# A hybrid decoder trunk in f32: new numbers for the model that orders the instructions, and VectorE in place of GpSimd

## The chip, the cores and the metric

The kernel runs on one core of a Trainium2 chip. The metric is device time in microseconds (us) of one execution; lower is better. The core's engines run their own instruction streams in order and meet through semaphores: TensorE (PE in the rows, PEld its weight loads), VectorE (DVE), ScalarE (ACT), GpSimd (POOL) and SyncE (SP), which here issues the weight transfers.

## The reference

Two layers, each a half-step SwiGLU network, a mixing stage of three branches with gates, and a second half-step SwiGLU network. 256 tokens, model width 1024, everything float32.

```python
for l in range(DEPTH):                       # DEPTH = 2
    h = rms_norm(x, ffn1_norm[l])
    x = x + 0.5 * swiglu(h, ffn1_w_gate[l], ffn1_w_up[l], ffn1_w_down[l])     # hidden 2816
    h = rms_norm(x, mix_norm[l])
    (u, q_b, c_kv, q_i, k_i, w_i, q_c, k_c, v_c, f_c, g_a, g_b, g_c) = split(h @ w_in[l])
    a = s5_branch(u, ...)                    # diagonal state space, 256 wide
    b = dsa_branch(q_b, c_kv, q_i, k_i, w_i, ...)   # 6 heads; an indexer keeps the 64 best keys of a query
    c = fox_branch(q_c, k_c, v_c, f_c)       # 6 heads, attention with forgetting
    merged = sigmoid(g_a) * (a @ w_branch_ssm) + sigmoid(g_b) * (b @ w_branch_dsa) + sigmoid(g_c) * (c @ w_branch_fox)
    x = x + merged @ w_out[l]
    h = rms_norm(x, ffn2_norm[l])
    x = x + 0.5 * swiglu(h, ffn2_w_gate[l], ffn2_w_up[l], ffn2_w_down[l])
return rms_norm(x, final_norm)
```

## The kernel before, in words

**Weights.** All weight matrices are read in the order that `plan` writes down, in units of two tiles of 128 rows by up to 512 columns. SyncE loads a unit into `raw` (four buffers). ScalarE copies it, rounded, into `hi` (`feed_hi`), another engine subtracts to get the rest, `lo = raw - hi` (`feed_lo`). The activations are split the same way (`h0h` and `h0l`, `bh` and `bl`, ...). TensorE then does three matmuls per tile and token half, hi by high part, lo by high part, hi by low part, into the accumulators `ps_acc`. These weight matmuls are nearly all of TensorE's work.

**Small work.** What lies between the big products (the state space scan, the indexer with its top 64, attention, the transposes of a norm) is written as Python generators. Their matmuls go to four scratch banks `ps_t`. `attend` works through three pairs of heads: scores (8 matmuls `ps_t<-kdT,qbT` for the sparse branch, `ps_t<-kcT,qcT` for the forgetting one), four reductions with the bias on VectorE (`st<-ps_t,bm` or `fm`), four exponentials with their sums on ScalarE (`st<-st,mn`), a reciprocal (`ri`), four scalings (`st<-st,ri`), two groups of three transposes (`ps_t<-ident,st`), two copies to `pt`, the value product (`ps_t<-pt,vd` or `pt,vs`), and its split into `bh` (ScalarE) and `bl` (VectorE).

**Who decides the order.** The program is written once, by this Python code, and runs in that order on each engine. `Clock` keeps a planned time for each engine, advanced by `Clock.cost` for every instruction. After each weight tile `Trunk.tick` looks through the generators and advances one, if what it waits for is ready by the planned time and if VectorE and ScalarE are planned no more than `BACKLOG` = 1.25 us past TensorE:

```python
if not self.blocked(g) and self.when(g) <= t["pe"] + EAGER and max(t["dve"], t["act"]) <= now + self.backlog[g]:
    self.step(g)
```

`Trunk.finish` runs given generators to their end and puts no weight matmul between their steps. `mix` calls it for the sparse attention before the product `branch dsa 0`, for the forgetting attention before `branch fox 0`, for the scan before `glu`, and for the transposes of the merged gates before each half of `w_out`. The mixing stage goes through `ORDER`: gate dsa 0, dsa 1, fox 0, fox 1, ssm 0, branch dsa 0, branch fox 0, gate ssm 1, glu, branch dsa 1, ssm 0, fox 1, ssm 1; then come `w_out` and the second network. "Gate" is a product of 1024 by 512 from `h`; "branch" a product of 256 or 384 by 512 from a branch's result, which VectorE multiplies with the gate (`gate<-gate,ps_acc`) and adds to the other branches (`gate<-gate`).

**GpSimd's share.** In the mixing stage a `lo` goes to GpSimd when VectorE is planned over 1 us past TensorE and GpSimd is not (`SPILL`), and so does a gate sum that is not the last one of its half. These are 34 `lo` and 8 gate sums in the two layers. GpSimd also adds the biases of attention (`bm`, `fm`).

All compute instructions stand in the profile at one line, that of the call in `Engine.__getattr__` (L193 before, L212 in the changed kernel), so rows are told apart by their tiles.

Of the kernel before, what the change touches and what calls it, by code (L numbers as in the profile page):

```python
# [9 lines left out]
F32 = mybir.dt.float32  # L10
# [3 lines left out]
OP = mybir.AluOpType  # L14
# [12 lines left out]
HD = 64  # L27
# [35 lines left out]

FEED, PACE = 0.3, 25.0

SPILL = 1.0, 1.5

T_BANKS = 4


# [4 lines left out]
def plan(a):  # L75
# [40 lines left out]
    for l in range(L):  # L116
        ffn(l, "ffn1")
        mix(l)
        ffn(l, "ffn2")
# [3 lines left out]
class Clock:  # L123
# [3 lines left out]
    def __init__(self):  # L127
        self.t = dict.fromkeys(("pe", "dve", "act", "pool", "dma"), 0.0)
        self.done = {}

    def ready(self, ap, eng=None):
        t, by = self.done.get(ap.tensor.name, (0.0, eng))
        return t + (SAME if by == eng else LATENCY)

    def put(self, eng, cost, outs, ins):
        start = max([self.t[eng]] + [self.ready(x, eng) for x in ins])
        self.t[eng] = start + cost
        for x in outs:
            done = start + cost + (1.8 if eng == "dma" else 0)
            self.done[x.tensor.name] = max(self.done.get(x.tensor.name, (0.0, eng)), (done, eng))  # L140
# [4 lines left out]
    def late(self, eng, cost, out, src):  # L145
        self.t[eng] += 1.0
        self.done[out.tensor.name] = max(self.t[eng], self.ready(src)) + cost + 3.0, "dma"

    @staticmethod
    def cost(eng, op, out, aps, kw):  # L150
        n = 1
        for d in out.shape[1:]:
            n *= d
        if eng == "pe":
            if op == "transpose":
                return 0.107
            return ((4 if aps[1].shape[0] > HD else 2) if aps[1].dtype == F32 else 1) * max(n / 2380, out.shape[0] / 1200)
        scalars = sum(x.shape[1:] == (1,) or list(x.shape[1:]) == [1] for x in aps[2:])
        if eng == "act":
            return 0.05 + n / 1200 + 0.045 * scalars + (0.13 if "accum_out" in kw else 0)  # L160
        if eng == "pool":
            return 0.14 + n * (2.15e-3 if op == "tensor_tensor" else 3.4e-3 if scalars else 1.15e-3)
        if op == "tensor_tensor_reduce":
            scalars = 0
        if op in ("max", "match_replace"):
            n = max(x.shape[-1] for x in aps)
        fast = op in ("tensor_scalar", "tensor_copy", "memset") and not any("ps_" in x.tensor.name for x in aps)
        return 0.07 + n * (0.52e-3 if fast else 1.04e-3) + 0.06 * scalars


class Engine:
# [3 lines left out]
    def __getattr__(self, op):  # L175
        f = getattr(self.eng, op)

        def call(*args, **kw):
            aps = [x for x in list(args) + list(kw.values()) if isinstance(x, bass.AP)]
            if op == "dma_start":  # L180
                n = 4
                for d in args[0].shape:
                    n *= d
                if self.name == "sp":
                    self.clock.put("dma", n / 360e3, aps[:1], aps[1:])
                else:
                    self.clock.late(self.name, n / 360e3, aps[0], aps[1])
            elif aps:
                outs = aps[:1] + [x for k, x in kw.items() if k == "accum_out"]
                if op == "tensor_tensor_reduce":  # L190
                    outs.append(aps[-1])
                self.clock.put(self.name, Clock.cost(self.name, op, aps[0], aps, kw), outs, aps[1:])
            return f(*args, **kw)  # L193

        return call
# [14 lines left out]
class Trunk:  # L210
    def __init__(self, ctx, tc, a, out):
        self.clock = Clock()  # L212
        self.tc, self.nc, self.a, self.out = tc, Engines(tc.nc, self.clock), a, out
        self.ctx = ctx
        nc = self.nc
        pool = lambda **kw: ctx.enter_context(tc.tile_pool(**kw))

        self.const = pool(name="const", bufs=1, side="right")
        self.rawp = pool(name="raw", bufs=RAW_BUFS, side="right")
        self.small = pool(name="small", bufs=2, side="right")  # L220
        self.hpool = pool(name="h", bufs=1, side="left")
        self.piecep = pool(name="piece", bufs=1, side="left")
        self.accp = pool(name="acc", bufs=4, space=PSUM)
        self.tp = pool(name="tps", bufs=T_BANKS, space=PSUM)
        self.dram = pool(name="scratch", bufs=2, space=DRAM)
        self.tlive, self.tcount = {}, 0
        self.bg, self.wait, self.rank, self.due, self.backlog = [], {}, {}, {}, {}
        self.spill = False

        self.units = plan(a)  # L230
        self.raw, self.split_tiles, self.freed = {}, {}, {}
        self.n_dma = self.n_hi = self.n_lo = self.n_used = 0
# [53 lines left out]
    def feed(self):  # L286

        now, ready = self.clock.t["pe"] + FEED, self.clock.ready
        while self.n_hi < min(self.n_used + HI_AHEAD, self.n_dma) and ready(self.raw[self.n_hi]) <= now:
            self.feed_hi(self.n_hi + 1)  # L290
        while self.n_lo < min(self.n_used + LO_AHEAD, self.n_hi) and ready(self.split_tiles[self.n_lo]) <= now:
            self.feed_lo(self.n_lo + 1)
# [40 lines left out]
    def feed_lo(self, upto):  # L333
        nc = self.nc
        while self.n_lo < min(upto, len(self.units)):
            i = self.n_lo
            _, nk, n = self.units[i]
            self.feed_hi(i + 1)
            src, hi = self.raw.pop(i)[:, :nk, :n], self.split_tiles[i]
            lo = self.piecep.tile([P, 2, 512], F32R, tag="lo", name="lo", bufs=LO_AHEAD + 1)  # L340
            t = self.clock.t
            eng = nc.gpsimd if self.spill and t["dve"] > t["pe"] + SPILL[0] and t["pool"] < t["pe"] + SPILL[1] else nc.vector
            eng.tensor_tensor(lo[:, :nk, :n], src, hi[:, :nk, :n].bitcast(F32), op=OP.subtract)
            self.split_tiles[i] = (hi, lo)
            self.freed[i] = self.clock.ready(lo)
            self.n_lo += 1
            self.feed_dma(i + 1 + RAW_BUFS)
# [320 lines left out]
    def mix(self, l, nxt):  # L668
        nc, tc = self.nc, self.tc
        a = self.a  # L670
# [3 lines left out]
        with tc.tile_pool(name="mix", bufs=1, side="left") as pool:  # L674
# [72 lines left out]
            gate, merged, left = {}, [None, None], [3, 3]  # L747
            mgens = []
            self.new = [None, None]
            for kind, name, d in ORDER:  # L750
                if kind == "gate":
                    g = gate[name, d] = pool.tile([P, 2, 512], F32, tag="gate", name="gate", bufs=5)
                    pg = self.acc()
                    for k0 in (0, 4):
                        self.mm_tok(pg, self.hx, k0, 4, 512, 0, 7)
                    for t in range(2):
                        nc.scalar.activation(g[:, t], pg[t], AF.Tanh, scale=rhalf[:, t:t + 1])
                    continue
                if kind == "glu":
                    self.finish(gen_s)  # L760
                    self.ssm_T = self.glu()
                    continue
                if name != "ssm":
                    self.finish(*((gen_x,) if name == "dsa" else (gen_g, gen_f)))
                hi, lo = getattr(self, f"{name}_T")
                nk = BRANCH_K[name]
                pb = self.acc()
                self.mm_tok(pb, lambda k: (hi[:, k], lo[:, k]), 0, nk, 512, 0, nk - 1)
                g = gate[name, d]
                left[d] -= 1  # L770
                for t in range(2):
                    nc.vector.scalar_tensor_tensor(g[:, t], g[:, t], 1.0, pb[t], op0=OP.add, op1=OP.mult)
                    if merged[d] is not None:
                        m = merged[d][:, t]
                        (nc.gpsimd if left[d] else nc.vector).tensor_tensor(m, m, g[:, t], op=OP.add)
                if merged[d] is None:
                    merged[d] = g
                if not left[d]:
                    self.new[d] = self.new_hT(d)
                    mgens.append(self.spawn(self.norm_T(merged[d], None, self.new[d]), -1))  # L780
# [593 lines left out]
    def run(self):  # L1374
        nc, tc, a = self.nc, self.tc, self.a
# [13 lines left out]
        for l in range(L):  # L1389
            with tc.tile_pool(name="prep", bufs=1, side="right") as pp:  # L1390
# [17 lines left out]
                gens.append(self.spawn(self.prep_layer(l, pp, *gens[:1]), 0, PREP))  # L1408
                self.ffn(C_MIX + 8 * l)
                self.finish(*gens)  # L1410
            self.spill = True
            self.mix(l, C_FFN2 + 8 * l)
            self.spill = False
            if l == L - 1:
                self.fn, self.y = self.late("fin", [P, D]), self.late("y", [P, 2, D])
                nc.gpsimd.dma_start(self.fn, a["final_norm"].rearrange("(o d) -> o d", o=1).partition_broadcast(P))
# [73 lines left out]
```

## Time and profile before

| | |
|---|---|
| device time, median of 3 runs | 1224.71 us (1224.34 to 1225.38) |
| the profiled execution | 1230.51 us |
| its span, first to last instruction | 1228.7 us |
| mean granted TensorE clock (1 is 2.4 GHz) | 0.979 |
| TensorE busy | 1177.6 us, 96% of the span |
| VectorE, ScalarE, GpSimd busy | 804.6, 601.8, 197.9 us |

The busy times are sums over the span; engines work beside each other. The profiled execution is 5.80 us longer than the median, of which 1.8 us lie outside its span. The granted clock has two levels in the rows, 1.00 and 0.50 (2.4 and 1.2 GHz).

### The profile page before, as it was taken

To read this page: it belongs to the slowest core of one execution; us is meant where nothing else is said; L and a number is where in the kernel's file an instruction comes from. 1 tells how busy PE (TensorE), PEld (TensorE's weight loads), DVE (VectorE), ACT (ScalarE), POOL (GpSimd) and SP (SyncE) were. 2 spreads that over 40 slices of the span, in tenths; PEclk is the share of its full clock that TensorE was granted. 3 is DMA by queue.
4 is the path that set the end of the run, shared out by engine and by line. 5 is a ranking of instruction groups with operands and counts; after the bars stand their busy time and mean duration, and the time that the engine had idled before them with its cause. 6 is when DMAs were issued, how large, how long until landed. Compare 5 with 4: busy or idle time off the path is not lost.

```text
span 1228.7 us, 16525 instructions
## 1 busy us (share of the span) xinstructions
PE 1177.6 (96%) x5976; PEld 986.1 (80%) x5976; DVE 804.6 (65%) x1335; ACT 601.8 (49%) x883; POOL 197.9 (16%) x192
## 2 busy tenths in 40 slices
PE   5999999997999999999999999998899999999996
PEld 4887888896868788888888888888777778888885
DVE  6987555699656775555576655557985576555554
ACT  4444444643665464444455445445365545544442
POOL 4116000153401380000000000012450130000000
PEclk8999999898999999999999999999899999999998
DMA  7765465444435656647655656554543455665661
GB/s 238 219 186 166 142 217 165 142 138 128 147 103 175 200 182 188 188 121 241 189 177 168 176 155 213 188 151 130 163 146 106 145 192 179 202 185 166 197 191 67
DMA packets 114898, 208.07 MB, mean 169 GB/s; under 512 B 7454, under 2 KB 26544, under 8 KB 114816
## 3 DMA queue, kind: packets, MB, share of 16 engines
q1 hardware_dynamic: 113024, 202.80, 53.1%
q0 software_dynamic: 1504, 3.81, 1.1%
q8 instruction: 47, 0.77, 0.3%
q10 hardware_dynamic: 288, 0.39, 0.1%
q14 instruction: 35, 0.29, 0.1%
HBM read 205.91 MB, written 1.07 MB: 168 GB/s over the span
## 4 chain that ended last, share of the span: by engine, by line
PE 85%; DVE 10%; ACT 2%; issue 1%; DMA 1%; SPq 0%; DVEq 0%; ACTq 0%
PE ps_acc L193 78%; PE ps_t L193 7%; DVE lo L193 2%; DVE score L193 2%; DVE gate L193 1%; DMA raw<-in_ffn_w_gate_dram 1%; DVE ft L193 1%; DVE m L193 1%; ACT u L193 1%; ACT hi L193 1%; DVE state L193 1%; ACT vT L193 0%; DVE rsqt L193 0%; DVE g L193 0%; SPq L193 0%
## 5 line engine op out<-in xcount | busy, mean ns | idle before, releaser
L193 ACT ACTIVATE hi<-raw 128x1024 fp32r<-128x1024 f32 (+3 forms) x415 | 410.9, 991 | 467.7 <-PE ps_acc L193 397.3
L193 DVE TENSOR_TENSOR lo<-raw,hi 128x1024 fp32r<-128x1024 f32 (+4 forms) x381 | 445.6, 1173 | 291.0 <-PE ps_acc L193 245.3
L193 PE MATMUL ps_acc<-hi,h0h 128*128 128x512 f32 (+3 forms) x544 | 218.1, 401 | 5.7 <-ACT hi L193 5.6
L193 PE MATMUL ps_acc<-lo,h0h 128*128 128x512 f32 (+3 forms) x544 | 210.0, 386 | 6.7 <-DVE lo L193 6.7
L193 PE MATMUL ps_acc<-hi,h0l 128*128 128x512 f32 (+3 forms) x544 | 209.7, 385 | 0.0
L193 PE MATMUL ps_acc<-hi,h1h 128*128 128x512 f32 (+3 forms) x544 | 209.6, 385 | 0.0
L193 PE MATMUL ps_acc<-hi,h1l 128*128 128x512 f32 (+3 forms) x544 | 204.8, 376 | 0.0
L193 PE MATMUL ps_acc<-lo,h1h 128*128 128x512 f32 (+3 forms) x544 | 204.7, 376 | 0.0
L193 PE MATMUL ps_acc<-hi,ath 128*128 128x512 f32 x352 | 138.0, 392 | 0.0
L193 PE MATMUL ps_acc<-hi,atl 128*128 128x512 f32 x352 | 137.1, 390 | 0.0
L193 PE MATMUL ps_acc<-lo,ath 128*128 128x512 f32 x352 | 137.0, 389 | 0.0
L193 PEld LDWEIGHTS ps_acc<-lo,h0h 128*128 128x128 f32 x544 | 106.0, 195 | 24.7 <-DVE lo L193 7.9
L193 PEld LDWEIGHTS ps_acc<-hi,h0h 128*128 128x128 f32 x544 | 105.8, 195 | 24.2 <-ACT hi L193 6.2
L193 PEld LDWEIGHTS ps_acc<-hi,h0l 128*128 128x128 f32 x544 | 105.8, 194 | 20.1 <-DVE h0l L193 0.6
L193 PEld LDWEIGHTS ps_acc<-hi,h1h 128*128 128x128 f32 x544 | 103.2, 190 | 19.7 <-issue 2.6
L193 PEld LDWEIGHTS ps_acc<-hi,h1l 128*128 128x128 f32 x544 | 103.0, 189 | 18.2
L193 PEld LDWEIGHTS ps_acc<-lo,h1h 128*128 128x128 f32 x544 | 103.2, 190 | 17.1 <-issue 0.5
L193 POOL TENSOR_TENSOR lo<-raw,hi 128x1024 fp32r<-128x1024 f32 (+3 forms) x34 | 72.9, 2154 | 193.7 <-PE ps_acc L193 99.3
L193 PEld LDWEIGHTS ps_acc<-hi,atl 128*128 128x128 f32 x352 | 66.1, 188 | 13.9
L193 PEld LDWEIGHTS ps_acc<-lo,ath 128*128 128x128 f32 x352 | 66.1, 188 | 13.3
L193 PEld LDWEIGHTS ps_acc<-hi,ath 128*128 128x128 f32 x352 | 66.1, 188 | 13.3
L193 POOL DMA_DIRECT2D wuk<-in_dsa_w_uk_dram x4 | 2.2, 560 | 459.6 <-PE ps_acc L193 358.4
(281 smaller groups left out, 1360.1 us busy)
## 6 DMA issues: line engine op xcount, KB each, us to landing
raw<-in_ffn_w_down_dram SPq DMA_DIRECT2D x88, 512.0 KB, 4.2
raw<-in_ffn_w_up_dram SPq DMA_DIRECT2D x80, 512.0 KB, 3.6
raw<-in_ffn_w_gate_dram SPq DMA_DIRECT2D x79, 512.0 KB, 3.6
raw<-in_w_in_dram SPq DMA_DIRECT2D x56, 512.0 KB, 3.5
raw<-in_w_out_dram SPq DMA_DIRECT2D x16, 512.0 KB, 3.8
raw<-in_ffn_w_gate_dram SPq DMA_DIRECT2D x18, 256.0 KB, 2.8
raw<-in_ffn_w_up_dram SPq DMA_DIRECT2D x16, 256.0 KB, 2.8
raw<-in_w_in_dram SPq DMA_DIRECT2D x16, 256.0 KB, 2.8
```

The source lines that it names most:

```text
L193: return f(*args, **kw)
```

## The change

The numbers of `Clock.cost` are replaced for all four compute engines. `Clock.shared` and a list `held` are new: they let the plan hold a VectorE instruction back while a GpSimd instruction that reads the same ports is planned, and the other way round. `SPILL` goes: every `lo` is VectorE's, and so is every gate sum. The core of the diff:

```diff
     def put(self, eng, cost, outs, ins, shared=False):
         start = max([self.t[eng]] + [self.ready(x, eng) for x in ins])
+        if shared:
+            for a, b in self.held["pool" if eng == "dve" else "dve"]:
+                if a <= start < b:
+                    start = b
+            self.held[eng] = self.held[eng][-8:] + [(start, start + cost)]
         self.t[eng] = start + cost
...
         if eng == "pe":
...
-            return ((4 if aps[1].shape[0] > HD else 2) if aps[1].dtype == F32 else 1) * max(n / 2380, out.shape[0] / 1200)
+            if aps[1].dtype == F32:
+                return (1 if aps[1].shape[0] > HD else 0.5) * (0.01 + max(n, out.shape[0]) / 600)
+            return 0.0135 + max(n / 2400, out.shape[0] / 1200)
...
         if eng == "act":
-            return 0.05 + n / 1200 + 0.045 * scalars + (0.13 if "accum_out" in kw else 0)
+            return 0.2 + n / 1205 + 0.03 * scalars
...
-        return 0.07 + n * (0.52e-3 if fast else 1.04e-3) + 0.06 * scalars
+        return 0.155 + n * (0.52e-3 if fast else 1.04e-3) + (0.06 * scalars if n > 16 else 0)
+
+    @staticmethod
+    def shared(eng, op, aps):
+
+        if eng == "pool":
+            return op != "memset"
+        ins = [x for x in aps[1:] if "ps_" not in x.tensor.name and x.shape[1:] != (1,) and list(x.shape[1:]) != [1]]
+        fast = op in ("tensor_scalar", "tensor_copy") and len(ins) == len(aps) - 1 and "ps_" not in aps[0].tensor.name
+        return eng == "dve" and (fast or len(ins) > 1)
...
-            t = self.clock.t
-            eng = nc.gpsimd if self.spill and t["dve"] > t["pe"] + SPILL[0] and t["pool"] < t["pe"] + SPILL[1] else nc.vector
-            eng.tensor_tensor(lo[:, :nk, :n], src, hi[:, :nk, :n].bitcast(F32), op=OP.subtract)
+            nc.vector.tensor_tensor(lo[:, :nk, :n], src, hi[:, :nk, :n].bitcast(F32), op=OP.subtract)
...
-                        (nc.gpsimd if left[d] else nc.vector).tensor_tensor(m, m, g[:, t], op=OP.add)
+                        nc.vector.tensor_tensor(m, m, g[:, t], op=OP.add)
```

The new numbers move instructions in all of the mixing stage, in both layers alike. The first place is TensorE at the end of gate ssm 0 and the start of branch dsa 0 (`bh` and `bl` are the split result of the sparse attention). Before, one product follows the other:

```order
L193 MATMUL ps_acc<-hi,h1h 128x512
L193 MATMUL ps_acc<-lo,h1h 128x512
L193 MATMUL ps_acc<-hi,h1l 128x512
L193 MATMUL ps_acc<-hi,bh 128x512
L193 MATMUL ps_acc<-lo,bh 128x512
L193 MATMUL ps_acc<-hi,bl 128x512
```

In the changed kernel, TensorE has this between them; the scores of the first pair alone stand earlier, among the gate's matmuls:

```order
L212 MATMUL ps_t<-ident,st 128x128 x3
L212 MATMUL ps_t<-kdT,qbT 128x256 x2
L212 MATMUL ps_t<-kdT,qbT 128x128 x2
L212 MATMUL ps_t<-ident,st 128x128 x3
L212 MATMUL ps_t<-pt,vd 64x256 x2
L212 MATMUL ps_t<-pt,vd 64x128 x2
L212 MATMUL ps_t<-ident,st 128x128 x6
L212 MATMUL ps_t<-pt,vd 64x256 x2
L212 MATMUL ps_t<-pt,vd 64x128 x2
L212 MATMUL ps_t<-kdT,qbT 128x256 x2
L212 MATMUL ps_t<-kdT,qbT 128x128 x2
...
L212 MATMUL ps_t<-ident,st 128x128 x6
```

Where three dots stand, four scores of the first forgetting pair follow, and behind the last row the third value product and then the first matmul with `bh`. Before, the three value products stood 79 and 49 rows apart among the gates' weight matmuls, the last one 74 rows ahead of the end of gate ssm 0.

The second place is TensorE between branch dsa 0 and branch fox 0. Before, their matmuls, which have the same names, follow each other without a break; in the changed kernel the forgetting attention, of which only the scores of two pairs stand earlier, is here as one piece:

```order
L212 MATMUL ps_acc<-hi,bl 128x512
L212 MATMUL ps_t<-ident,st 128x128 x6
L212 MATMUL ps_t<-pt,vs 64x256 x2
L212 MATMUL ps_t<-pt,vs 64x128 x2
L212 MATMUL ps_t<-ident,st 128x128 x6
L212 MATMUL ps_t<-pt,vs 64x256 x2
L212 MATMUL ps_t<-pt,vs 64x128 x2
L212 MATMUL ps_t<-kcT,qcT 128x256 x2
L212 MATMUL ps_t<-kcT,qcT 128x128 x2
L212 MATMUL ps_t<-ident,st 128x128 x6
L212 MATMUL ps_t<-pt,vs 64x256 x2
L212 MATMUL ps_t<-pt,vs 64x128 x2
```

So six steps of attention stand without a weight matmul among them, where none did. On VectorE, in both places, `bl` of a pair stands ahead of the reductions of the next pair (of two of the four, for the second forgetting pair).

The third place is VectorE at the end of the mixing stage, from the multiplication of branch fox 1 to the first half of `w_out` (`h0l` is the low part of the first transposed half of the merged gates). Before:

```order
L193 SCALAR_TENSOR_TENSOR gate<-gate,ps_acc 128x512 x2
L193 TENSOR_TENSOR lo<-raw,hi 128x1024
L193 SCALAR_TENSOR_TENSOR h0l<-ps_t,h0h 128x512 x2
L193 SCALAR_TENSOR_TENSOR gate<-gate,ps_acc 128x512
L193 TENSOR_TENSOR gate<-gate 128x512
L193 SCALAR_TENSOR_TENSOR gate<-gate,ps_acc 128x512
L193 TENSOR_TENSOR gate<-gate 128x512
L193 TENSOR_TENSOR lo<-raw,hi 128x1024
```

And in the changed kernel:

```order
L212 SCALAR_TENSOR_TENSOR gate<-gate,ps_acc 128x512
L212 TENSOR_TENSOR gate<-gate 128x512
L212 SCALAR_TENSOR_TENSOR gate<-gate,ps_acc 128x512
L212 TENSOR_TENSOR gate<-gate 128x512
L212 TENSOR_TENSOR lo<-raw,hi 128x1024
L212 SCALAR_TENSOR_TENSOR gate<-gate,ps_acc 128x512
L212 TENSOR_TENSOR gate<-gate 128x512
L212 SCALAR_TENSOR_TENSOR gate<-gate,ps_acc 128x512
L212 TENSOR_TENSOR gate<-gate 128x512
L212 SCALAR_TENSOR_TENSOR h0l<-ps_t,h0h 128x512 x2
```

The two sums of fox 1 have come over from GpSimd, and `h0l` has moved from ahead of the last branch's four instructions to behind them. On TensorE the eight transposes for `h0h` and `h0l` moved with it, behind the last weight matmul of the last branch. At the start of the second network a like thing is seen: `h0l` stood between the two pairs of additions to `x`, and stands now behind both, on ScalarE `h0h` behind the squares of the second pair.

## Rows read from the trace of the kernel before

**Rows 1.** The page, busy time of each engine over the span.

```profile
PE 1177.6 (96%) x5976; PEld 986.1 (80%) x5976; DVE 804.6 (65%) x1335; ACT 601.8 (49%) x883; POOL 197.9 (16%) x192
```

**Rows 2.** Waits of TensorE: us in total, times, longest us.

```profile
PE ps_t L193 <- DVE qbT L193: 9.8, 2, 6.1
...
PE ps_t L193 <- ACT qk L193: 5.0, 2, 2.5
PE ps_t L193 <- ACT st L193: 4.1, 2, 2.0
PE ps_t L193 <- DVE cn L193: 3.5, 2, 1.9
PE ps_t L193 <- DVE ft L193: 3.3, 2, 1.7
PE ps_t L193 <- DVE gate L193: 3.2, 4, 0.8
```

**Rows 3.** Busy time by window; the last columns: granted clock, DMA share, GB/s.

```profile
238.60:245.40 6.80, 5.78 (x24) 5.39 (x25) 2.84 (x6) 2.90 (x5) 0.00 (x0) 0.50 0.02 6
245.40:286.40 41.00, 34.47 (x272) 33.35 (x270) 40.31 (x98) 16.86 (x27) 18.93 (x9) 1.00 0.42 125
286.40:296.60 10.20, 7.08 (x22) 5.44 (x23) 9.94 (x26) 2.67 (x9) 3.39 (x3) 0.50 0.43 145
344.40:347.80 3.40, 3.40 (x9) 2.66 (x10) 2.00 (x12) 3.04 (x11) 0.00 (x0) 0.51 0.49 154
680.00:720.00 40.00, 40.00 (x182) 33.15 (x181) 22.43 (x26) 18.79 (x21) 0.00 (x0) 1.00 0.61 175
842.80:846.20 3.40, 3.40 (x12) 3.40 (x12) 3.37 (x7) 1.06 (x1) 0.00 (x0) 0.50 0.04 6
```

**Rows 4.** The page, GpSimd's `lo`: busy us, mean ns, idle before.

```profile
L193 POOL TENSOR_TENSOR lo<-raw,hi 128x1024 fp32r<-128x1024 f32 (+3 forms) x34 | 72.9, 2154 | 193.7 <-PE ps_acc L193 99.3
```

**Rows 5.** Groups of VectorE by form, 228 to 420 us: busy us, mean ns.

```profile
L193 DVE TENSOR_TENSOR lo<-raw,hi 128x1024 fp32r<-128x1024 f32 x32 | 41.8, 1310 | 20.8 <-PE ps_acc L193 18.4 <-ACT hi L193 1.7 <-issue 0.6
L193 DVE SCALAR_TENSOR_TENSOR gate<-gate,ps_acc 128x512 f32<-128x512 f32 x12 | 7.8, 679 | 0.1
L193 DVE TENSOR_TENSOR gate<-gate 128x512 f32<-128x512 f32 x4 | 6.3, 1564 | 0.4
...
L193 DVE COPY pt<-ps_t 128x384 f32<-128x384 f32 x7 | 3.9, 553 | 0.3 <-PE ps_t L193 0.2
```

**Rows 6.** Timeline: start us, us, engine, line, op, tiles, count.

```profile
287.88 1.65 PE L193 MATMUL ps_t<-kdT,qbT 64*128 64x256 f32 x8 [6.13 <-DVE qbT L193]
...
311.09 0.49 PE L193 MATMUL ps_t<-ident,st 128*128 128x128 f32 x3
...
311.50 0.92 PE L193 MATMUL ps_t<-kdT,qbT 64*128 64x256 f32 x8
...
312.57 0.29 DVE L193 CUSTOM_DVE_ANT_0 st<-ps_t,bm 128x128 f32<-128x128 f32 x1
...
312.96 0.40 ACT L193 ACTIVATE st<-st,mn 128x128 f32<-128x128 f32 x1
...
314.64 0.19 ACT L193 ACTIVATION_READ_ACCUMULATOR st<-st,mn 128x1 f32 x1
...
342.35 0.17 DVE L193 RECIPROCAL ri<-rs 128x4 f32<-128x4 f32 x1
342.55 0.40 ACT L193 ACTIVATE st<-st,ri 128x128 f32<-128x128 f32 x1 [0.91 <-DVE ri L193]
...
343.00 0.55 PE L193 MATMUL ps_t<-ident,st 128*128 128x128 f32 x3 [2.04 <-ACT st L193]
...
352.91 0.87 PE L193 MATMUL ps_t<-pt,vd 128*64 128x256 f32 x8
...
353.83 0.39 ACT L193 ACTIVATE bh<-ps_t 128x256 fp32r<-128x256 f32 x1
...
354.25 0.42 DVE L193 TENSOR_TENSOR bl<-ps_t,bh 128x256 fp32r<-128x256 f32 x1 [0.94 <-ACT bh L193]
```

More of the change, by code (lines that the diff above doesn't have):

```diff
@@ L64 @@
 FEED, PACE = 0.3, 25.0
-SPILL = 1.0, 1.5
 T_BANKS = 4
@@ L129, in __init__ @@
         self.done = {}
+        self.held = {"dve": [], "pool": []}
     def ready(self, ap, eng=None):
@@ L133, in ready, with put @@
         return t + (SAME if by == eng else LATENCY)
-    def put(self, eng, cost, outs, ins):
+    def put(self, eng, cost, outs, ins, shared=False):
         start = max([self.t[eng]] + [self.ready(x, eng) for x in ins])
+        if shared:
[3 more added lines that the diff above has]
+            self.held[eng] = self.held[eng][-8:] + [(start, start + cost)]
         self.t[eng] = start + cost
@@ L156, in cost @@
                 return 0.107
-            return ((4 if aps[1].shape[0] > HD else 2) if aps[1].dtype == F32 else 1) * max(n / 2380, out.shape[0] / 1200)
+            if aps[1].dtype == F32:
+                return (1 if aps[1].shape[0] > HD else 0.5) * (0.01 + max(n, out.shape[0]) / 600)
+            return 0.0135 + max(n / 2400, out.shape[0] / 1200)
         scalars = sum(x.shape[1:] == (1,) or list(x.shape[1:]) == [1] for x in aps[2:])
         if eng == "act":
-            return 0.05 + n / 1200 + 0.045 * scalars + (0.13 if "accum_out" in kw else 0)
+            return 0.2 + n / 1205 + 0.03 * scalars
         if eng == "pool":
-            return 0.14 + n * (2.15e-3 if op == "tensor_tensor" else 3.4e-3 if scalars else 1.15e-3)
+            return 0.16 + n * (2.2e-3 if op == "tensor_tensor" else 3.4e-3 if scalars else 0.8e-3 if op == "memset" else 2e-3)
         if op == "tensor_tensor_reduce":
@@ L166, in cost @@
             n = max(x.shape[-1] for x in aps)
-        fast = op in ("tensor_scalar", "tensor_copy", "memset") and not any("ps_" in x.tensor.name for x in aps)
-        return 0.07 + n * (0.52e-3 if fast else 1.04e-3) + 0.06 * scalars
+        if op == "tensor_tensor_scan":
+            return 0.155 + n * 2e-3
+        fast = op in ("tensor_scalar", "tensor_copy", "memset") and not any("ps_" in x.tensor.name for x in aps) and n > 128
+        return 0.155 + n * (0.52e-3 if fast else 1.04e-3) + (0.06 * scalars if n > 16 else 0)
[6 more added lines that the diff above has]
+        return eng == "dve" and (fast or len(ins) > 1)
 class Engine:
@@ L191, in call @@
                     outs.append(aps[-1])
-                self.clock.put(self.name, Clock.cost(self.name, op, aps[0], aps, kw), outs, aps[1:])
+                self.clock.put(self.name, Clock.cost(self.name, op, aps[0], aps, kw), outs, aps[1:],
+                               Clock.shared(self.name, op, aps))
             return f(*args, **kw)
@@ L227, in __init__ @@
         self.bg, self.wait, self.rank, self.due, self.backlog = [], {}, {}, {}, {}
-        self.spill = False
         self.units = plan(a)
@@ L1410, in run @@
                 self.finish(*gens)
-            self.spill = True
             self.mix(l, C_FFN2 + 8 * l)
-            self.spill = False
             if l == L - 1:
```

## The prediction

> **What bounds the kernel now.** I read the page's busy times first: TensorE works 1177.6 of 1228.7 us, no other engine over two thirds [rows 1]. So time can only be won where TensorE stands still or runs slowly, and lost where it is made to. TensorE's waits come next. Apart from the start of the program, which the new order leaves as it was, they are all for small work of the mixing stage: 9.8, 5.0, 4.1, 3.5 and 3.3 us over both layers, together 25.7, and 3.2 for the gate sums ahead of `w_out` [rows 2]. Then the windows around these waits: they show a granted clock of 0.50, the 1.2 GHz level, behind a wait or a thinning of the work, with 5.78, 7.08 and 3.40 us of TensorE work in them in layer 0 and 3.40 in the first of layer 1 [rows 3]; layer 1 repeats the second and third. That is 30.1 us of work at half speed, so 15.1 us lost. At most 25.7 + 15.1 = 40.8 us can come back from the mixing stages; the gate wait is taken separately below.
>
> VectorE is the engine that is late there: 40.31 of 41.0 us busy from 245.4 to 286.4, with GpSimd busy 18.93 beside it [rows 3]. It works slower beside GpSimd. A gate sum, 128x512, takes 1564 ns on the mean, the multiplication of the same size 679 [rows 5].
>
> **The change, part by part.** I give the cost for one layer; both layers' mixing stages have the same new order.
>
> *What it removes.* GpSimd's 34 `lo` took 72.9 us [rows 4]. On VectorE the 17 of a layer cost at most 1.31 each, 22.3, and the four gate sums .68 each, as the multiplication of that size [rows 5]; 25 us more instructions per layer, partly repaid by undisturbed ones. The order also puts off much small work: the first sparse scores come 184 rows later on TensorE. So VectorE and ScalarE have room early, and I expect the five waits of the stage's first half to go. I take the whole 40.8 us as returned, the most that the rows allow; the lower end is that half stays, 20.4.
>
> *A, the sparse block.* What is put off has to be done by `finish`, with nothing for TensorE to do between. At the end of gate ssm 0 nearly three pairs of attention now stand in one piece (the first `order` rows). Each pair's value product depends on a chain through three engines. From the start of one value product: .92 to `bh`, .42 to `bl`, .42 for `bl` itself, then the next pair's first reduction, which stands behind it on VectorE, .39 to its exponential, 1.87 from the first exponential to the end of the last sum (312.96 to 314.83), .20 for the reciprocal, .45 from scaling to transposes, about .5 for the other head's scaling, .55 for its transposes, .55 for the copy: 6.3 us, of which I take 6.2, as some of it starts early [rows 5, 6]. The third pair's scores stand behind the second value product, and its reductions start 1.07 after them (311.50 to 312.57), so it takes about 6.4. With 2.8 for what is left of the first pair and .87 for the last product: 16.3 us at full clock. At half clock scores take 1.65 instead of .92 [rows 6]; I add .9 a pair, which is 19.0. TensorE's own work in it at full clock is six groups of transposes (.41 from one start to the next), three scores (.92) and three value products (.87), 7.8 us. The block therefore adds 8.5 us at full clock, 11.2 at half. I take 11.2: waits of 2.48 to 6.13 us are what stands ahead of the half clock in the rows, and this block is made of such waits.
>
> *B, the forgetting block.* The same ahead of branch fox 0, with only one pair of scores inside: 2.8 + 5.2 + 6.4 + .87 = 15.3 at full clock (5.2, as two reductions with their exponentials are done earlier), and as it begins slowly, 19.4. TensorE's own work: 6 x .41 + .92 + 3 x .87 = 6.0. It adds 9.3 or 13.4; I take 13.4.
>
> No row of before shows such a block. From below, if the pairs overlapped fully, each would cost what its busiest engine does, about 3 us (four exponentials 1.87, scalings, `bh`), and both blocks would add almost nothing; `bl` ahead of the next reductions excludes that. From above, GpSimd's bias additions may disturb VectorE in them; with one and a half times what a gate sum lost (1564 - 679 = 885 ns) that is 1.3 to 1.4 a block.
>
> *C, the clock behind the blocks.* The rows have 5.78 and 7.08 us of work at 0.50 behind waits. I take 6 us behind each block, 3 lost each: 6.0. The Trainium skill says, in TensorE: Matmul & The Clock Gate, section HAM oscillation, that a stream of matmuls broken by waits falls back to half rate and that every stretch starts cold again; the trace agrees, with 0.50 from 286.4 to 296.6 behind a wait of 6.13 us. By that rule gathering work into blocks costs twice, as I have it; by the full-clock reading (below) it would cost the waits alone.
>
> *D, ahead of `w_out`.* The last branch is 12 weight matmuls of .22 (40.0 us for 182 rows [rows 3]), 2.6 us. In them VectorE now does fox 1's four instructions (4 x .68 = 2.7) and a `lo` (1.31), so it is 1.4 us behind at their end; the last branch's four follow (2.7), and the transposes of both halves stand behind them. TensorE waits about 4.0 instead of 1.6 (four gate waits, 3.2 in two layers [rows 2]): +2.4. Behind such a wait I take 3.40 us of work at half clock: +1.7.
>
> *E, at the second network's start.* `h0l` behind two more additions and a square, three operations of 128x512 at about .65: +1.9.
>
> Sum for a layer: 11.2 + 13.4 + 6.0 + 2.4 + 1.7 + 1.9 = 36.6. For two 73.2, less 40.8: +32.4 us. The durations come from the profiled execution of 1230.51 us (span 1228.7), which would become 1262.9; set against the median, 1224.7 + 32.4 = **1257 us**.
>
> **The rivals.**
>
> *The clock holds.* The blocks' own matmuls may be enough to keep the clock at 1.00. Then A is 8.5, B 9.3, C nothing, D 2.4 and E 1.9: 22.1, twice 44.2, less 40.8: +3.4, about 1228. For it: the waits for `cn` [rows 2], one of which lies in the window from 245.4 to 286.4, leave that window at 1.00 [rows 3]. Against it: 0.50 behind the wait of 6.13 [rows 3, 6].
>
> *Faster: VectorE is no longer disturbed, and the blocks are cheap.* This is one mechanism: with GpSimd quiet, the 128-wide scalings and sums run at their undisturbed length, small work lands where the new plan puts it, and each block is covered. If all of the blocks' cost disappeared, 1224.7 - 40.8 = 1184; it decides for faster when the new cost is under 20.4 us a layer, just below the 22.1 that full clock gives. For it speaks the gate sum's 1564 against 679 ns. Against it: no weight matmul stands in the blocks, so nothing covers them. The Trainium skill, SBUF — State Buffer, section Who interferes with whom, calls the ports that VectorE shares with GpSimd an exclusive lock: an instruction that comes second waits for the whole of the other. The trace agrees, with that 1564 beside 679; by that rule taking GpSimd out gains whatever the order is.
>
> *VectorE is overloaded.* If its 25 us more a layer find no room, the `lo` come late and weight matmuls wait. It was busy 40.31 of 41.0 us in the worst stretch. If some 20 us a layer come onto the path: 1257 + 40 = 1297. Against it: small work of that stretch has been put off.
>
> *The change does nothing:* gains and blocks even out, within 2.4 us of before; it needs a cost of 20.4 a layer, by chance alone.
>
> **How the numbers follow.** Forecast .70; clock holds .14; VectorE overloaded .07; faster .06; even .03. The forecast's own range is 1244 (half of what half clock adds to A and B, and half of C: 6.4 a layer less) to 1277 (1.4 more in each block, and a third of the 40.8 not returned: 5.6 + 13.6 more). To hold 8 in 10 it takes in the clock rival: 1227 to 1277. About 0.2%, 2.4 us, is what a measurement of this kernel can tell from no change. Faster by more: .06, and .02 of the clock rival, .08. Within: .03, and .04 of the clock rival, .07. Slower: .85.
>
> **What would show each step.** The waits for `qk`, `cn`, `kdT`/`qbT` and `ft` gone or smaller; the gate sums on VectorE near .69. Ahead of branch dsa 0 and branch fox 0 a stretch of 16 to 20 us without a weight matmul, in which TensorE waits for `pt`, `st` and `mn`, with the clock at 0.50 in and behind it; some 4 us of waiting for `gate` ahead of `w_out`; a mean clock below 0.979. The prediction is wrong if the blocks last under 10 us, if the clock stays at 1.00, or if waits for `lo` come up among the gates.

## The result, and the profile after

The changed kernel takes 1252.08 us (1250.54 to 1253.74, 4 runs), against 1224.64 us: 1.0223 times as long, 95% interval 1.0206 to 1.0241. Forecast were 1257 us and slower. The profiled executions differ by 23.2 us (1253.74 against 1230.51); their spans, 1251.9 and 1228.7, by the same.

The page's first row, the counterpart of [rows 1]:

```profile
PE 1189.2 (95%) x5976; PEld 993.5 (79%) x5976; DVE 798.3 (64%) x1381; ACT 602.6 (48%) x879; POOL 101.2 (8%) x150
```

GpSimd's work is halved, and VectorE, with 46 instructions more, is busy 6.3 us less. TensorE does the same 5976 instructions in 11.6 us more. So half of the 23.2 us shows as longer TensorE work, and the other 11.6 as idle time. The split is rough: a row of several matmuls can hold a wait inside it, as the second value product below does. The waits of TensorE (us in total, times, longest), to be held against [rows 2]:

```profile
PE ps_t L212 <- ACT st L212: 23.9, 8, 3.7
...
PE ps_acc L212 <- DVE h0l L212: 6.2, 2, 3.1
...
PE ps_t L212 <- DVE st L212: 5.9, 5, 1.6
PE ps_acc L212 <- ACT h0h L212: 3.5, 4, 1.5
```

The rows for `qbT`, `qk`, `cn`, `ft` and `gate` are gone. What stands there now is attention: 23.9 + 5.9 us of waiting for scaled scores (`st`), and 6.2 + 3.5 for the transposed halves ahead of `w_out` (`h0l`) and of the second network (`h0h`). VectorE's groups, 228 to 445 us, answer to [rows 5]:

```profile
L212 DVE TENSOR_TENSOR lo<-raw,hi 128x1024 fp32r<-128x1024 f32 x46 | 58.1, 1269 | 25.7 <-PE ps_acc L212 15.7 <-issue 8.0 <-ACT hi L212 1.7
L212 DVE SCALAR_TENSOR_TENSOR gate<-gate,ps_acc 128x512 f32<-128x512 f32 x12 | 8.0, 679 | 0.0
L212 DVE TENSOR_TENSOR gate<-gate 128x512 f32<-128x512 f32 x8 | 5.5, 692 | 0.3
```

A gate sum takes 692 ns where it took 1564, and VectorE has time to spare, 25.7 us ahead of the large `lo` alone. It is not the bound. The two blocks of layer 0 in windows (us, busy time of each engine; the last three columns are granted clock, DMA share and GB/s):

```profile
333.94:339.00 5.06, 3.47 (x23) 1.94 (x21) 2.15 (x8) 2.32 (x7) 0.00 (x0) 1.00 0.26 95
340.20:346.60 6.40, 5.26 (x24) 3.45 (x26) 2.64 (x6) 1.57 (x5) 1.41 (x2) 0.51 0.00 0
347.00:349.60 2.60, 0.40 (x6) 0.19 (x2) 1.54 (x11) 2.14 (x9) 0.00 (x0) 1.00 0.00 0
350.40:353.60 3.20, 3.20 (x14) 1.91 (x13) 1.11 (x5) 1.60 (x6) 0.00 (x0) 0.55 0.03 5
353.80:357.20 3.40, 3.40 (x20) 2.52 (x19) 1.58 (x6) 2.00 (x6) 1.42 (x2) 1.00 0.33 72
363.50:373.50 10.00, 7.20 (x30) 4.32 (x28) 3.42 (x12) 2.65 (x8) 0.00 (x0) 0.50 0.00 0
377.60:380.80 3.20, 3.20 (x13) 1.82 (x12) 0.67 (x2) 0.86 (x3) 0.00 (x0) 0.54 0.00 0
381.00:384.40 3.40, 3.40 (x17) 2.75 (x16) 2.40 (x4) 1.58 (x2) 0.00 (x0) 1.00 0.22 49
418.40:421.80 3.40, 3.40 (x12) 2.67 (x12) 1.22 (x2) 0.50 (x1) 0.00 (x0) 0.54 0.42 122
```

The busy times are those of PE, PEld, DVE, ACT and POOL. In the 6.4 us from 340.2 TensorE has 5.26 us of work, at half clock, VectorE 2.64 and ScalarE 1.57; in the 2.6 us from 347.0 TensorE has 0.40, the other two 1.54 and 2.14. It is a chain, in which one engine waits for the other. One turn of it, from the second value product of the sparse block to the next transposes, on the timeline:

```profile
343.09 2.25 PE L212 MATMUL ps_t<-pt,vd 128*64 128x256 f32 x8
...
345.27 1.47 PE L212 MATMUL ps_t<-kdT,qbT 64*128 64x256 f32 x8
345.38 0.38 ACT L212 ACTIVATE bh<-ps_t 128x256 fp32r<-128x256 f32 x1 [2.34 <-PE ps_t L212]
345.79 0.42 DVE L212 TENSOR_TENSOR bl<-ps_t,bh 128x256 fp32r<-128x256 f32 x1 [2.05 <-ACT bh L212]
...
346.89 0.29 DVE L212 CUSTOM_DVE_ANT_0 st<-ps_t,bm 128x128 f32<-128x128 f32 x1 [0.67 <-PE ps_t L212]
...
349.32 0.40 ACT L212 ACTIVATE st<-st,ri 128x128 f32<-128x128 f32 x1 [0.24 <-DVE ri L212]
...
349.78 0.45 PE L212 MATMUL ps_t<-ident,st 128*128 128x128 f32 x1 [2.38 <-ACT st L212]
```

The value product takes 2.25 us here where it took .87 [rows 6], the scores 1.47 instead of .92. Not all of this is the clock: the first value product of the block, at a granted clock of 1.00, takes 1.58 (at 335.93, shown below), as the third of its eight matmuls starts .7 us behind the first, where it was .3 before. Then ScalarE (`bh`), VectorE (`bl` and the reductions), ScalarE (exponentials), VectorE (reciprocal) and ScalarE (scaling) follow until the transposes at 349.78.

### The profile page after: what moved, and what is told of

Same layout as the page of the kernel before. It is cut to its first block, busy times and chain, and to the rows that moved or that the text cites. A ratio compares the mean times of both kernels' runs of the same rounds, so it can differ in the third digit from the quotient of the medians.

```text
span 1251.9 us, 16455 instructions
## 1 busy us (share of the span) xinstructions
PE 1189.2 (95%) x5976; PEld 993.5 (79%) x5976; DVE 798.3 (64%) x1381; ACT 602.6 (48%) x879; POOL 101.2 (8%) x150
## 5 line engine op out<-in xcount | busy, mean ns | idle before, releaser
L212 DVE TENSOR_TENSOR lo<-raw,hi 128x1024 fp32r<-128x1024 f32 (+3 forms) x415 | 473.4, 1147 | 282.6 <-PE ps_acc L212 209.0
L212 PE MATMUL ps_acc<-hi,h0h 128*128 128x512 f32 (+3 forms) x544 | 213.6, 393 | 9.8 <-ACT hi L212 6.2
L212 PE MATMUL ps_acc<-lo,h0h 128*128 128x512 f32 (+3 forms) x544 | 207.2, 381 | 5.9 <-DVE lo L212 5.9
L212 PE MATMUL ps_acc<-hi,h1h 128*128 128x512 f32 (+3 forms) x544 | 206.4, 379 | 0.0
L212 PEld LDWEIGHTS ps_acc<-lo,h1h 128*128 128x128 f32 x544 | 102.5, 188 | 17.2 <-issue 0.2
L212 PE MATMUL ps_t<-ident,st 128*128 128x128 f32 x72 | 17.5, 380 | 30.1 <-ACT st L212 23.9
L212 DVE SCALAR_TENSOR_TENSOR act<-ps_acc,rstd,s 128x512 f32<-128x512 f32 (+1 forms) x48 | 32.1, 705 | 18.6 <-PE ps_acc L212 18.6
```

## The experiments

Ratios are to the kernel before, measured beside each of the three groups of runs: 1225.75 us for the kernels of experiments 1, 2 and the 0.07 of experiment 3, 1226.70 for its other two, the first kind of fillers and the first kernel of experiment 5, 1226.15 for the rest. The intervals behind the ratios are of 95%.

**1. The engine move alone, and the numbers alone.** The first kernel is the one before with the move:

```diff
-            t = self.clock.t
-            eng = nc.gpsimd if self.spill and t["dve"] > t["pe"] + SPILL[0] and t["pool"] < t["pe"] + SPILL[1] else nc.vector
-            eng.tensor_tensor(lo[:, :nk, :n], src, hi[:, :nk, :n].bitcast(F32), op=OP.subtract)
+            nc.vector.tensor_tensor(lo[:, :nk, :n], src, hi[:, :nk, :n].bitcast(F32), op=OP.subtract)
...
-                        (nc.gpsimd if left[d] else nc.vector).tensor_tensor(m, m, g[:, t], op=OP.add)
+                        nc.vector.tensor_tensor(m, m, g[:, t], op=OP.add)
```

> The kernel before with every lo and every gate sum on VectorE, and its old cost numbers. The order has no block of sparse attention left and one short piece of five rows of forgetting attention. Theory (the loss comes from the order that the new numbers make, with attention in pieces that nothing covers): 1205 to 1228 us, not slower than before; no waits of 2 to 4 us for st ahead of branch dsa 0 and branch fox 0. Rival (VectorE is overloaded by the 17 lo and 4 sums that a layer adds to it): 1240 us or more, with TensorE waiting for lo or gate among the gates.

1224.58 us, 0.9995 (0.9983 to 1.0008): no change. The waits of the first half are smaller, but the order differs, and it has waits of its own:

```profile
PE ps_acc L193 <- DVE h0l L193: 6.4, 2, 3.2
...
PE ps_t L193 <- ACT pt L193: 5.0, 6, 2.0
PE ps_t L193 <- ACT st L193: 3.4, 2, 1.7
PE ps_t L193 <- ACT qk L193: 3.4, 2, 2.0
```

VectorE is not overloaded by the work: no wait for `lo` but those of the program's start. The second kernel is the changed one with the two edits above undone.

> The changed kernel with its new cost numbers and its model of shared ports, but with the rule that sends lo to GpSimd and the gate sums on GpSimd as before. The order has the forgetting block whole (11 rows) and the sparse one in part (6 rows instead of 16). Theory (order): 1238 to 1255 us, most of the loss stays: the forgetting block's 15 us a layer, and some 6 of the sparse one. Rival (the engine move makes the loss): 1220 to 1230.

1231.92 us, 1.0047 (1.0031 to 1.0064). Slower by 6 us, so the numbers cost time without the move, but less than I expected: the stretch with the 11 rows of the forgetting block lasts 14.7 us here (354.94 to 369.59), where it lasts 21.5 in the changed kernel. The two halves of the change do not add up: 0 and +6 us alone, +27 together. The order points to the reason: 16 rows stand in the sparse block instead of 6. With VectorE's 25 us more a layer, its planned time should lie further behind TensorE's, and more attention is left to `finish`; the planned times themselves are not on record.

**2. How far VectorE may be behind.** The changed kernel with one number changed:

```diff
-TICK, BACKLOG, PREP, EAGER = 1.5, 1.25, 0.0, -0.5
+TICK, BACKLOG, PREP, EAGER = 1.5, 8.0, 0.0, -0.5
```

> The changed kernel with one number changed: BACKLOG 8 us in place of 1.25, so that generators go on although VectorE or ScalarE is planned far behind. The order has no attention block; small work stands earlier. Theory (order): the 32 us of a layer's blocks and their neighbours go; 1190 to 1228, as waits of the first half may come back in part. Rival (the blocks are not the cause, VectorE's load is): 1245 or more.

1225.66 us, 0.9987 (0.9968 to 1.0006). The blocks are gone, and 26 us with them, but the old waits are back; TensorE's in total:

```profile
PE ps_acc L212 <- DVE lo L212: 11.3, 6, 5.3
PE ps_t L212 <- DVE qbT L212: 8.8, 2, 4.4
```

About 5 of the 11.3 for `lo` lie outside the program's start. The clock has a share too. Behind the wait for `qbT` in layer 0 it stands at 0.50 for 23.9 us, with TensorE busy nearly all the time:

```profile
282.72:306.62 23.90, 23.40 (x89) 20.57 (x90) 12.00 (x37) 7.07 (x22) 6.86 (x6) 0.50 0.22 67
```

Between too little and too much small work ahead of the gates there must be a better place.

**3. VectorE's planned cost.** One line of the changed kernel, the planned cost of most instructions of VectorE, whose fixed part is 0.155 us:

```diff
-        return 0.155 + n * (0.52e-3 if fast else 1.04e-3) + (0.06 * scalars if n > 16 else 0)
+        return 0.04 + n * (0.52e-3 if fast else 1.04e-3) + 0.06 * scalars
```

In the first of the three kernels 0.07 stands there, which makes it the line of the kernel before, in the others 0.10 and 0.04. The condition `n > 16` goes in all three, so they differ from each other in one number, but from the changed kernel in two things.

> The changed kernel with VectorE's old cost formula alone (0.07 us per instruction in place of 0.155). The order has the sparse attention spread again and a forgetting block of 8 rows (three value products, scores earlier) in place of 11. Theory (order; VectorE's fixed cost is what puts small work off): the sparse block's 12 us a layer go, the forgetting one costs 12 to 15 still: 1224 to 1236. Rival (VectorE's load, not its planned cost): 1245 or more.

> The changed kernel with VectorE's planned cost per instruction 0.10 us in place of 0.155 (0.07 ran at 1216). By the order the forgetting block is whole (11 rows), the sparse one has 6 rows (two pairs, scores done). Theory (the order's blocks set the time): between the two, 1224 to 1240. Rival (the loss grows evenly with the number, or comes from another of the new numbers): 1216 as with 0.07, or 1245 and more.

> The changed kernel with VectorE's planned cost per instruction 0.04 us. The order has no attention block at all. Theory (blocks): the 1.5 us waits for st that 0.07 still has go: 1206 to 1217, if small work put earlier does not make the old waits for qk, cn and qbT come back; with them 1217 to 1228. Rival (VectorE's load is what counts): 1245 or more.

| planned cost, us | rows in the two blocks, sparse and forgetting | the two stretches without a weight matmul, layer 0, us | time, us | ratio to before (95%) |
|---|---|---|---|---|
| 0.155 (the change) | 16 and 11 | 19.4 and 21.5 | 1252.08 | 1.0223 (1.0206 to 1.0241) |
| 0.10 | 6 and 11 | 7.6 and 13.8 | 1226.30 | 0.9992 (0.9979 to 1.0005) |
| 0.07, the line of before | spread but for the last pair, and 8 | 4.7 and 8.7 | 1216.12 | 0.9923 (0.9910 to 0.9936) |
| 0.04 | none | 0.3 and 0 | 1203.63 | 0.9811 (0.9796 to 0.9826) |

The stretches are read from the timelines of the profiled executions. The kernels compute the same; only the order differs. The time follows the blocks, and the rival of an overloaded VectorE falls: all of its work is there in each of the four. With 0.07 the kernel ran better than I expected (1224 to 1236), and with 0.04 a little better too. The waits of the last in the mixing stages, beyond those for `h0l`, are 2.4 us in both layers:

```profile
PE ps_acc L212 <- DVE h0l L212: 7.4, 2, 3.7
...
PE ps_t L212 <- ACT qk L212: 1.9, 2, 1.0
PE ps_t L212 <- ACT st L212: 0.5, 2, 0.3
```

**4. The clock in the blocks.** Extra matmuls that nobody reads, first behind every step of the blocks, then only ahead of a pair's first transposes:

```diff
                 i, ps = yield from self.bank()
+                if e == 0 and self.fill:
+                    fp, (xh, _) = self.acc(1)[0], self.hx(0)
+                    for _ in range(self.fill):
+                        self.tc.nc.tensor.matmul(fp[:, :T], xh[:, :P], xh[:, :T], start=True, stop=True)
                 for b in range(3):
```

This is the second kind; `fill` is 14 while the two attentions are finished, else 0. The first kind has two such matmuls in `finish`, behind each step of a generator.

> The changed kernel, order unchanged, with two extra matmuls of 256 columns, whose result nobody reads, behind every step that the two attention blocks make: 76 in the sparse block, some 8 us of TensorE work. They add work and remove none. Theory (half of the blocks' price is the clock, which is 0.50 in stretches of them): the granted clock stays at 1.00 in the blocks, the sparse one shrinks from 19.5 to about 17 us and the forgetting one from 21.4 to about 17: 1234 to 1244 us. Rival (only the chain of waits counts, the clock doesn't matter): 1250 to 1262.

1253.78 us, 1.0215 (1.0199 to 1.0231): not what I expected. The mean clock rose from 0.972 to 0.990, but the blocks of layer 0 last 21.4 and 20.1 us in place of 19.4 and 21.5, as each step of the chain now stood behind fillers. That run could not tell the clock from the fillers' own time.

> The changed kernel, order unchanged, with 14 extra matmuls of 256 columns (some 1.5 us, read by nobody) at one point of each pair in the two blocks: ahead of its first transposes, where TensorE waits 2.4 to 3.7 us. The earlier filler kept the clock at 1.00 but stood in the way of every step (1253.8 us); this one stands only in the long waits. Theory (half clock costs some 5 us a layer in and behind the blocks): 1236 to 1246. Rival (the chain of waits alone sets the blocks' length): 1249 to 1256, with the clock at 1.00 all the same.

1242.60 us, 1.0133 (1.0114 to 1.0151), as expected. The windows of the sparse block's end, of the stretch between, and of the forgetting block:

```profile
340.00:354.00 14.00, 12.83 (x76) 9.27 (x77) 7.15 (x28) 7.06 (x23) 1.48 (x3) 0.88 0.05 6
354.00:361.00 7.00, 5.38 (x33) 4.12 (x34) 5.52 (x12) 2.82 (x7) 4.89 (x4) 1.00 0.57 178
361.00:380.00 19.00, 16.25 (x100) 12.74 (x99) 11.09 (x32) 8.87 (x22) 0.00 (x0) 1.00 0.14 42
```

With 140 more matmuls the kernel is 9.5 us faster than without, and the blocks of layer 0 last 17.6 and 17.2 us: 4.7 us a layer is what the half clock costs at the least, the fillers' own delay not counted. They don't lift it quite: 3.4 us of the sparse block still run at half clock. The rest of the blocks' price is the chain.

**5. The transposes ahead of `w_out`.** One line makes `finish` do those of the first half ahead of the last branch:

```diff
+                if (name, d) == ("ssm", 1):
+                    self.finish(mgens[0])
                 hi, lo = getattr(self, f"{name}_T")
```

On the kernel with 0.07, and on the changed kernel itself:

> The kernel with VectorE's cost 0.07 and one line more: the transposes of the first merged half are finished ahead of the last branch product, so that h0l stands ahead of that branch's four instructions on VectorE. Theory (term D: h0l behind them makes TensorE wait 3.2 us a layer, and run at half clock behind it): 1206 to 1213 us against 1216, with no wait for h0l over 1 us. Rival (the wait only moves, to the transposes ahead of the last branch or to the gate sums behind it): 1214 to 1219.

> The changed kernel with the transposes of the first merged half ahead of the last branch, nothing else; its blocks stay. Theory (term D adds to the blocks, 1.7 us of wait over before and 1.6 of clock, and gives back its whole wait of 3.3): 1241 to 1246 against 1252.1. Rival: 1249 to 1253, as the time behind the blocks is made up elsewhere.

1207.44 us, 0.9841 (0.9827 to 0.9855), against 1216.12: 8.7 off. And 1241.16 us, 1.0116 (1.0096 to 1.0136), against 1252.08: 10.9 off, 5.5 a layer, about what D measures below with its clock. In both no wait for `h0l` is left.

**6. The best of it, and what GpSimd's share costs there.**

> VectorE's planned cost 0.04 us (1203.6 alone) and the transposes of the first merged half ahead of the last branch (which took 8.7 us off the kernel with 0.07). Theory (the two act in different places and add up): 1193 to 1197, no wait of over 1 us in either mixing stage. Rival (the wait for h0l moves elsewhere in this order): 1199 to 1205.

1192.53 us, 0.9721 (0.9700 to 0.9742), a little under what I expected: faster than before and after, with a mean clock of 0.997. What is left of waits in the mixing stages:

```profile
PE ps_t L212 <- ACT qk L212: 1.7, 2, 1.0
...
PE ps_t L212 <- ACT st L212: 0.5, 2, 0.3
```

The last kernel has 0.04 and GpSimd's `lo` and gate sums as before (without the line of experiment 5):

> VectorE's planned cost 0.04 us, and the share of GpSimd (lo by the old rule, gate sums) as before the change. The order has no attention block. Against 1203.6 us, the same cost with all of it on VectorE, it prices the engine move in an order that covers attention. Theory (the move is a gain, as GpSimd's instructions slow VectorE's): 1210 to 1226, with early waits of 1 to 6 us for qbT, cn or qk back. Rival (the move is worth nothing, only the order counts): 1200 to 1207.

1225.13 us, 0.9989 (0.9975 to 1.0003), against 1203.63 with all of it on VectorE. Where the order covers attention the engine move is worth 21.5 us. This is the price of the share together with the order that the plan makes of it: the order differs as well, this kernel keeps the condition `n > 16`, and 25 us of its work in the mixing stages run at half clock, 7 in the kernel with 0.04. What the engines alone are worth was not measured. `qbT` and the gates are waited for again, and VectorE's own instructions are longer, the large `lo` 1434 ns where it takes 1225 in the kernel with 0.04, and a gate sum 1199 where it takes 692:

```profile
L214 DVE TENSOR_TENSOR lo<-raw,hi 128x1024 fp32r<-128x1024 f32 x36 | 51.6, 1434 | 17.2 <-PE ps_acc L214 7.7 <-ACT st L214 3.2 <-ACT hi L214 3.1
...
L214 DVE TENSOR_TENSOR gate<-gate 128x512 f32<-128x512 f32 x4 | 4.8, 1199 | 0.4
...
L212 DVE TENSOR_TENSOR lo<-raw,hi 128x1024 fp32r<-128x1024 f32 x46 | 56.1, 1225 | 19.8 <-PE ps_acc L212 10.8 <-issue 4.4 <-ACT hi L212 4.1
```

The last line is of the kernel with 0.04.

## Why the prediction was right, step by step

*What is removed:* right. All five waits of the first half went, and the half clock behind them; the stage's first 104 us in layer 0 have TensorE busy throughout at 1.00:

```profile
228.00:332.00 104.00, 104.00 (x641) 93.69 (x640) 83.21 (x190) 57.80 (x91) 8.88 (x9) 1.00 0.60 178
```

*A, the sparse block,* and *B, the forgetting block,* on TensorE's timeline in layer 0:

```profile
333.94 0.49 PE L212 MATMUL ps_t<-ident,st 128*128 128x128 f32 x3
...
335.93 1.58 PE L212 MATMUL ps_t<-pt,vd 128*64 128x256 f32 x8
341.19 1.95 PE L212 MATMUL ps_t<-ident,st 128*128 128x128 f32 x6 [3.68 <-ACT st L212]
...
353.37 0.51 PE L212 MATMUL ps_acc<-hi,bh 128*128 128x512 f32 x1
...
358.45 0.40 PE L212 MATMUL ps_acc<-hi,bl 128*128 128x512 f32 x1
360.25 0.30 PE L212 MATMUL ps_t<-ident,st 128*128 128x128 f32 x1 [1.40 <-DVE st L212]
...
368.38 1.54 PE L212 MATMUL ps_t<-ident,st 128*128 128x128 f32 x6 [2.80 <-ACT st L212]
...
376.79 1.25 PE L212 MATMUL ps_t<-ident,st 128*128 128x128 f32 x6 [3.10 <-ACT st L212]
...
380.16 0.68 PE L212 MATMUL ps_acc<-hi,bh 128*128 128x512 f32 x1
```

*A:* right. It lasts 19.4 us (333.94 to 353.37), in layer 1 the same, forecast 19.0; less TensorE's own 7.8 that is 11.6, forecast 11.2. The waits that the profile names, 3.68 and 2.38 us, and half of the 8.46 us of work at 0.51 and 0.55 make 10 of it; the rest lies inside rows, as in the value product at 335.93.

*B:* right in kind, too small in size. It lasts 21.5 us (from 358.68, where the next weight matmul would have stood, .23 us after the one at 358.45, to 380.16), in layer 1 20.9, forecast 19.4; less the 6.0 of its own work that is 15.2 on the mean, forecast 13.4. The prediction gives no working for its step from 15.3 at full clock to 19.4, and the upper end of its range adds up to 1276, not 1277. The price isn't one of these 11 rows in general: with 0.10 the same rows take 13.8.

*C, the clock behind the blocks:* wrong. 353.8 to 357.2 and 381.0 to 384.4 stand at 1.00. The half clock lies in the blocks and ends with them in layer 0, and in layer 1 about 1 us behind the second, so 0 to .5 in place of 6.0 us a layer.

*D, ahead of `w_out`:* right, with a smaller size: TensorE stands still for 3.3 us, not 4.0, and runs 3.40 us at 0.54 behind it as forecast. That it can be had back was shown by experiment 5. `h0h` came earlier than I had it; only the first matmul with `h0l` waits, 3.08 us:

```profile
413.93 0.68 DVE L212 SCALAR_TENSOR_TENSOR gate<-gate,ps_acc 128x512 f32<-128x512 f32 x1
...
416.58 1.28 DVE L212 SCALAR_TENSOR_TENSOR h0l<-ps_t,h0h 128x512 fp32r<-128x512 f32 x2
417.31 0.50 PE L212 MATMUL ps_acc<-hi,h0l 128*128 128x512 f32 x1 [3.08 <-DVE h0l L212]
```

*E, the second network:* 1.52 us of waiting for `h0h`, forecast 1.9.

Of the signs that the prediction named, waits for `pt`, `mn` and `gate` didn't come: TensorE waits for `st` in the blocks and for `h0l` ahead of `w_out`.

The sum by these rows, 11.6 + 15.2 + 0 + 1.7 + 1.7 + 1.5 = 31.7 a layer, is 63.4 for both, less 40.8: +22.6. Measured were +23.2 between the profiled executions. The same weight matmul in both kernels shows that the 40.8 came back whole. Here it is before the mixing stage of layer 0 and behind both blocks, first in the kernel before, then in the changed one:

```profile
235.15 0.34 PE L193 MATMUL ps_acc<-lo,h0h 128*128 128x390 f32 x1
...
377.02 0.39 PE L193 MATMUL ps_acc<-lo,bh 128*128 128x512 f32 x1
...
234.19 0.34 PE L212 MATMUL ps_acc<-lo,h0h 128*128 128x390 f32 x1
...
380.67 0.39 PE L212 MATMUL ps_acc<-lo,bh 128*128 128x512 f32 x1
```

The changed kernel is 0.96 us ahead and then 3.65 behind, so gains and blocks together cost 4.6 in layer 0, and in the same way 8.2 in layer 1 (836.19 and 974.84 against 844.97 and 991.80). Within 0.2 us that is A and B of the layer less the waits and half clock that the trace of before holds in it, 22.3 and 18.4 us.

So the mechanism was right but for C, and the 1257 is closer to 1252 than its terms are: C was too large by 12 us in both layers, A and B too small by 4.4, D and E too large by 2. The sum missed by 10, +32.4 against +22.6. Between the medians the change is +27, as the profiled execution of before lay 5.8 us over its median and that of the changed kernel only 1.7; this brought the forecast's time 4 us closer, and that is luck.

*The rivals.* The clock did not hold; where fillers held it nearly everywhere in the blocks (experiment 4) the kernel was still slower than before. VectorE was not overloaded. The move didn't gain whatever the order is: alone, with the old numbers, it was worth nothing (experiment 1). And the faster rival was the right one for another order: with the blocks gone the same work on the same engines takes 1203.63 us.

## What to carry to other kernels

A planner's cost number sets not only how well it foresees times; it moves the thresholds that are compared with them. That holds for good numbers too: for `bl`, 128x256, the formula of the change gives 0.155 + 256 x 1.04e-3 = 0.42 us, and 0.42 were measured, where the one with 0.04 gives 0.31, and its kernel runs 48 us faster. The costs of the change should make VectorE look further behind; a limit of 1.25 us, unchanged, then put attention off until a forced finish had to do it with nothing beside it. Change such numbers together with the limits, read the order for stretches without the main work before measuring, and test the engine move and the ordering apart: the move was worth nothing with the old numbers, cost 20 us with the new ones (1252.08 against 1231.92) and gained 21.5 with 0.04.

## What the runs showed that I had not expected

The clock of the changed kernel came back to 1.00 within the 3.4 us behind a block, or before it ended, where [rows 3] had 5.78 and 7.08 us of work at 0.50 behind the waits of before, and the kernel of experiment 2 had 23.40 behind a wait of 4.39 in layer 0 and 5.37 behind one of 4.38 in layer 1. What decides how long it stays low was not tested. And matmuls that nobody reads paid for themselves: 140 of them, in waits that were there anyway, took 9.5 us off.
